# The 20 slabs of w_in multiplied in fp32 instead of as pairs of fp32r halves

## The chip, the cores and the metric

One Trainium2 chip, one core. The metric is the device time of one execution in microseconds. TensorE (PE) multiplies, VectorE (DVE), ScalarE (ACT) and GpSimd (POOL) work element-wise, SyncE (SP) issues most of the loads.

## The reference

One step of a hybrid backbone (one layer, two groups of 128 tokens, width 1024). Both groups share all weights, so the kernel treats them as 256 columns of tokens.

```python
h = _rmsnorm(x, p["norm1_g"]) * (1.0 + sc1) + sh1
z = h @ p["w_in"] + p["b_in"]                  # 1024 x 5120
z_f, z_a, z_b, z_s, z_g = jnp.split(z, cuts, axis=-1)
br_f = _fourier_mix(z_f) @ p["w_four"]
br_c = _conformer_conv(z_a, z_b, ...) @ p["w_conv_out"]
y_s, finals = _s5_bidirectional(z_s, ...)      # two scans
gs = jax.nn.gelu(y_s)
y_s = gs * jax.nn.sigmoid(gs @ p["w_ssm_glu"] + p["b_ssm_glu"])
br_s = y_s @ p["w_ssm_out"]
mixed = (gate_f * br_f + gate_c * br_c + gate_s * br_s) @ p["w_out"]
x = x + g1 * mixed
x = x + g2 * _moe(h2, ...)                     # top 4 of 32 experts
```

## The kernel before

*Stages.* First come the adaLN modulation of the first norm and the tables of the S5 mixer, then the products with w_in, w_four, w_ssm_out, w_conv_out and w_out, with the three mixers between them, then the router, and then the 32 experts, one after the other, whose weights (12 slabs of 1 MB each) stream from HBM.

*Slabs.* Weights arrive as slabs of 1 MB (128 partitions x 2048 fp32) in slots `SL[i]`. `Ring` hands a free slot to the next load in a fixed order (`ring.add`); SP issues the loads in that order, each when its slot has become free (`ring.done`, `ring.give`; a slot named in `ring.drop` does not come back). The loads of w_in (20 slabs of 256 columns, keys `("in", c0)`) alternate with those of w_mod for the later modulation (`("m", ...)`). After the last slab of w_out come the experts' slabs.

*Order.* The stages before the experts are written as generators (`modulate`, `splitter`, `main_products`, `evacuate`, `fourier`, `conv`, `s5`, ...). A planner (`Sched`) with a cost for every operation advances, one instruction at a time, the generator whose next instruction can start soonest, with a small penalty by priority (`PRIO`). This happens while the program is built: on the chip each engine runs its own list in that order.

*The products with w_in.* The operands are fp32r, and each is written as a pair of tiles: `hi` is its copy in fp32r, and `lo` what is left when `hi` is subtracted from it. `modulate` writes h into xT (slot 20) and as the pair `hhi`, `hlo` (slots 4 and 5). `splitter` takes each slab in four units of 128x512: ACT copies a unit to `hi` (fp32r), and DVE or POOL, whichever the planner holds to be free sooner, subtracts for `lo`; `NW = 4` units may be ahead of the products. `main_products` then makes three products (`prod3`) for each block of 128 rows and 128 columns, in PSUM banks 0 and 1 in turn. `evacuate` reads a finished bank: ACT adds the bias, or makes the gates' sigmoid. The branches' weights (w_four, w_conv_out, w_ssm_out, six keys `("pr", i, h)`) and w_out (four slabs) go through the same splitter. All instructions made by `mm` have line 273, all of `tt` line 291, all of `act` line 304, those of `ts` lines 279 and 282.

*Order of the slabs.* Eight slabs of z come first (S5's two, Fourier's two, the convolution's four), then six times two gate slabs and half of one branch's output weights, in the order Fourier, S5, convolution; then w_out. S5 needs, besides its two slabs, tables of which DVE and POOL make parts (`tables_in`, `tables_out`), a scan of 16 steps on DVE whose states ACT copies, and a convolution kernel that goes out to HBM (`Kd`) and comes back in another layout. `fourier` keeps an intermediate in slot 20, after xT is no longer read there; `evacuate` accumulates the gated sum in it.

## Time and profile before

| | us |
|---|---|
| median of 3 runs (lowest, highest) | 1414.85 (1414.38, 1416.57) |
| profiled execution | 1418.22 |
| its span, first to last instruction | 1416.4 |
| busy in it: PE / PE's weight loads | 1243.9 / 655.7 |
| busy in it: DVE / ACT / POOL | 492.4 / 301.5 / 216.0 |
| HBM read | 472.61 MB |
| mean granted TensorE clock | 0.961 of full |

Full clock of TensorE is 2.4 GHz and the other level is 1.2 GHz, so a granted clock of 0.79 over a stretch is a mixture of the two. Busy shares hold for the whole span, in which stages with different limits follow each other. PE's weight loads (PEld) overlap its products. An engine's wait is put down to what ended it.

### The profile page before, as it was taken

Reading aid. Unit: us, or ns where it says so; the run is one execution under the profiler, and the core shown is the slowest. Engines: PE = TensorE matmul, PEld = TensorE weight load, DVE = VectorE, ACT = ScalarE, POOL = GpSimd, SP = SyncE. Lnnn points to the kernel's source line nnn. Section 1 sums busy time; section 2 is a strip of 40 time slices with the busy share of each in tenths; the row PEclk is TensorE's granted clock in tenths of the full one; section 3 lists DMA queues with packets and bytes.
Section 4 is the critical chain, followed back from the end, with each engine's and each line's share of the span. In section 5 each row is a group of like instructions: output and inputs, shape, how many; then the busy total and the mean of one; then the engine's idle time right before and its main releaser. Section 6 shows DMA issues by size and latency. Waiting matters only on the chain. (4 is left out here: it accounts for less than half of the span.)

```text
span 1416.4 us, 19588 instructions
## 1 busy us (share of the span) xinstructions
PE 1243.9 (88%) x7444; PEld 655.7 (46%) x7444; DVE 492.4 (35%) x839; ACT 301.5 (21%) x609; POOL 216.0 (15%) x183
## 2 busy tenths in 40 slices
PE   4596787899999999999989999999999989999994
PEld 3475686789833433334343433333334334343331
DVE  7949898897511111111111111111121111211113
ACT  4454344454311101011100101101011101111011
POOL 4555556565300000000000000000000000000001
PEclk9798899999999999999999999999999999999996
DMA  9563489558799999999998999998999994999990
GB/s 268 193 210 115 144 146 266 188 196 316 290 352 410 416 397 415 416 416 415 417 415 319 407 417 414 415 400 357 416 416 416 416 409 185 413 415 415 414 395 33
DMA packets 124834, 477.08 MB, mean 337 GB/s; under 512 B 11871, under 2 KB 49505, under 8 KB 90864
## 3 DMA queue, kind: packets, MB, share of 16 engines
q1 hardware_dynamic: 121744, 468.25, 85.3%
q0 software_dynamic: 2288, 5.76, 1.2%
q8 instruction: 120, 1.97, 0.6%
q10 hardware_dynamic: 624, 0.63, 0.1%
q14 instruction: 58, 0.48, 0.1%
HBM read 472.61 MB, written 1.61 MB: 335 GB/s over the span
## 5 line engine op out<-in xcount | busy, mean ns | idle before, releaser
L273 PE MATMUL pb<-sl,sl 128*64 128x512 f32 (+4 forms) x5344 | 951.3, 485 | 48.7 <-PEq L1644 13.1
L273 PEld LDWEIGHTS pb<-sl,sl 128*64 128x64 f32 (+2 forms) x5344 | 438.4, 152 | 521.8 <-issue 445.2
L304 ACT ACTIVATE sl<-sl 128x512 fp32r<-128x512 f32 (+4 forms) x211 | 120.8, 588 | 614.2 <-DVE sl L279 496.4
L291 POOL TENSOR_TENSOR sl<-sl,sl 128x512 fp32r<-128x512 f32 (+4 forms) x73 | 121.1, 1667 | 737.5 <-DVE sl L291 607.7
L279 DVE TENSOR_SCALAR sl<-pb 128x512 f32<-128x512 f32 (+1 forms) x35 | 23.7, 676 | 434.7 <-PE pb L273 434.7
L287 DVE SCALAR_TENSOR_TENSOR sl<-pb,wsl,sl 128x512 fp32r<-128x512 f32 x64 | 47.7, 750 | 310.5 <-ACT sl L304 309.3
L291 DVE TENSOR_TENSOR sl<-sl,sl 128x512 fp32r<-128x512 f32 (+3 forms) x107 | 105.6, 1001 | 30.1 <-ACT sl L304 27.7
L304 ACT ACTIVATE sl<-pb 128x512 f32<-128x512 f32 (+6 forms) x125 | 68.5, 585 | 199.2 <-PE pb L273 177.8
L262 PE MATMUL pb<-cst,sl 128*128 128x128 f32 (+2 forms) x354 | 57.4, 296 | 46.0 <-ACT sl L304 15.0
L304 ACT ACTIVATE sl<-pb,wsl 128x512 fp32r<-128x512 f32 x64 | 43.6, 687 | 199.6 <-PE pb L273 196.6
L273 PE MATMUL pb<-sl,PT 128*128 128x512 f32 x256 | 78.0, 428 | 0.5 <-PEq L1644 0.5
L273 PE MATMUL pb<-hb,sl 128*128 128x128 f32 x512 | 68.4, 289 | 7.9 <-DVE hb L291 7.5
L273 PEld LDWEIGHTS pb<-hb,sl 128*128 128x128 f32 x512 | 65.1, 200 | 18.3 <-ACT wsl L304 11.8
L262 PEld LDWEIGHTS pb<-cst,sl 128*128 128x128 f32 (+2 forms) x354 | 43.7, 158 | 63.0 <-issue 26.1
L318 POOL MEMSET sl<- 128x30 f32 (+6 forms) x15 | 2.8, 228 | 374.1 <-PEq L1644 373.8
L287 DVE SCALAR_TENSOR_TENSOR hb<-sl,taps,hb 128x256 f32<-128x256 f32 x90 | 55.5, 664 | 0.6
L273 PEld LDWEIGHTS pb<-sl,PT 128*128 128x128 f32 x256 | 46.2, 201 | 8.0 <-ACT sl L304 1.3
L291 POOL TENSOR_TENSOR sl<-PWT,sl 128x1024 f32<-128x1024 f32 x20 | 43.5, 2190 | 11.1 <-PE pb L273 6.2
L273 PEld LDWEIGHTS pb<-comb,hb 128*128 128x128 f32 x128 | 19.6, 207 | 44.6 <-DVE sl L279 41.9
L291 DVE TENSOR_TENSOR sl<-sl 128x512 f32<-128x512 f32 (+4 forms) x77 | 37.1, 500 | 4.1 <-ACT sl L304 0.5
L273 PE MATMUL pb<-comb,hb 128*128 128x1 f32 x128 | 22.0, 241 | 18.2 <-PEq L1644 16.4
L273 PE MATMUL pb<-ha,selb 128*64 128x512 bf16 (+1 forms) x140 | 21.3, 390 | 16.8 <-PEq L1644 14.4
(176 smaller groups left out, 547.0 us busy)
## 6 DMA issues: line engine op xcount, KB each, us to landing
sl<-w_gate_up SPq DMA_DIRECT2D x256, 1024.0 KB, 14.9
sl<-w_down SPq DMA_DIRECT2D x128, 1024.0 KB, 17.5
sl<-w_mod SPq DMA_DIRECT2D x24, 1024.0 KB, 7.2
sl<-w_in SPq DMA_DIRECT2D x20, 1024.0 KB, 11.1
sl<-w_out SPq DMA_DIRECT2D x4, 1024.0 KB, 6.9
sl<-md POOLq DMA_DIRECT2D x6, 512.0 KB, 6.9
sl<-w_four SPq DMA_DIRECT2D x2, 1024.0 KB
sl<-Kd SPq DMA_DIRECT2D x16, 128.0 KB, 9.2
```

The costliest lines, as they stand in the source:

```text
L262: return sch.op("P", 0.107 * in_.shape[0] / 128, [out], [in_], lambda: te.transpose(out, in_, ident[:in_.shape[0], :in_.shape[0]]))
L273: lambda: te.matmul(out, lhsT, rhs, start=start, stop=stop, skip_group_check=True))
L279: return sch.op(e, c, [o], ap, lambda: ENG[e].tensor_scalar(o, a, s1, None, op0=op0))
L287: lambda: ENG[e].scalar_tensor_tensor(o, a, sc, b, op0=op0, op1=op1))
L291: return sch.op(e, c, [o], [a, b], lambda: ENG[e].tensor_tensor(o, a, b, op=op))
L304: [a] + [x for x in (bias, scale) if hasattr(x, "tensor")], lambda: s.activation(o, a, func, **kw))
L318: return sch.op(e, size(o) * 0.9e-3 + 0.1, [o], [], lambda: ENG[e].memset(o, val))
```

## The change

h is written once, in fp32, into xT: ACT modulates one group of tokens and DVE the other. The pair `hhi`, `hlo` goes, and the splitter passes over the w_in slabs. `main_products` multiplies each w_in slab as it came, in fp32, one product for each block (16 for a slab), and gives the slot back after the last of them. Slot 4 belongs to the ring from the start. Slot 5 takes what the Fourier branch and the gated sum kept in slot 20, and slot 20 goes to the ring after the last product with w_in. `m1_transposes` no longer waits for the first split slab, and the planner's cost of an fp32r product is raised.

```diff
--- before.py
+++ after.py
@@ -264,7 +264,7 @@
         def mm(out, lhsT, rhs, start, stop=False):
             n, m = size(rhs), lhsT.shape[1]
             if lhsT.dtype != F32:
-                c = max(n, m) * 4.17e-4
+                c = max(n, m) * 4.6e-4
             elif m > 64:
                 c = max(n, m) * 1.667e-3
             else:
@@ -433,7 +433,7 @@
             dma("Y", BR[i].rearrange("g d p h -> g d (p h)"), A[n][0].rearrange("d g p h -> g d (p h)"))
         start(0, 1)
         start(2, 3)
-        start(6, 7, 8, 9)
+        start(6, 7, 4, 8, 9)
         dma("G", vrow[0:40], A["b_in"][0].rearrange("(k p) -> k p", p=128))
         for i, n in enumerate(("conv_dw_b", "conv_ln_g", "conv_ln_b", "ssm_d", "b_ssm_glu")):
             dma("G", vrow[40 + 4 * i:44 + 4 * i], A[n][0].rearrange("(k p) -> k p", p=128))
@@ -461,8 +461,6 @@
         R0 = [SL[15][:, 1024:1536], SL[15][:, 1536:2048]]
         modA = sm.tile([128, 2, 8, 2], F32, name="modA")
         pm = sm.tile([128, 4, 2], F32, name="pm")
-        hhi = new(4, F32R)[:, :].rearrange("p (k t) -> p k t", k=8)
-        hlo = new(5, F32R)[:, :].rearrange("p (k t) -> p k t", k=8)
 
         def adaln(key, bk):
             w = ring.get(key)
@@ -533,10 +531,10 @@
                 yield f"xT{b}"
                 for k in (2 * b, 2 * b + 1):
                     for g in range(2):
-                        yield act(hhi[:, k, 128 * g:128 * g + 128], xT[:, k, g], AF.Identity, bias=modA[:, 0, k, g:g + 1],
-                                  scale=modA[:, 1, k, g:g + 1])
-                        yield ts(xT[:, k, g], xT[:, k, g], modA[:, 1, k, g:g + 1], modA[:, 0, k, g:g + 1])
-                    yield tt(hlo[:, k], flat(xT[:, k]), fv(hhi[:, k]), OP.subtract)
+                        if g:
+                            yield ts(xT[:, k, g], xT[:, k, g], modA[:, 1, k, g:g + 1], modA[:, 0, k, g:g + 1])
+                        else:
+                            yield act(xT[:, k, g], xT[:, k, g], AF.Identity, bias=modA[:, 0, k, g:g + 1], scale=modA[:, 1, k, g:g + 1])
                     flags.add(f"hmod{k}")
                 if b == 3:
                     yield tr(PB[2][:, 0:64], vrow)
@@ -810,8 +808,6 @@
         def m1_transposes(js, banks):
             yield from need("xT", "R2", *(("m0",) if js[0] else ()))
             for j in js:
-                if j == 2:
-                    yield "in0"
                 yield f"T{j}"
                 for h in range(2):
                     for i in range(2):
@@ -1036,7 +1032,7 @@
 
         def fourier():
             yield from need("zf", "columns", "M10", "M11", "M12", "M13")
-            UV = SL[20][:, :].rearrange("p (j b c) -> p j b c", j=4, b=2)
+            UV = SL[5][:, :].rearrange("p (j b c) -> p j b c", j=4, b=2)
             for i in range(4):
                 for b in range(2):
                     yield mm(PB[6 + i % 2][:, b * 256:(b + 1) * 256], zf[:, i, b * 128:(b + 1) * 128], cst[:, C_DFT:C_DFT + 256],
@@ -1066,17 +1062,14 @@
             new(21, F32R)
             new(22, F32R)
             n = 0
-            for key in seq + [("out", q) for q in range(4)]:
-                for u in UNITS if key == seq[0] else range(4):
+            for key in [x for x in seq if x[0] == "pr"] + [("out", q) for q in range(4)]:
+                for u in range(4):
                     yield lambda: key in ring.ready and cnt["used"] >= n - NW + 1
                     sl = ring.get(key)
                     if key[0] == "out":
                         src = sl[:, u * 512:(u + 1) * 512].rearrange("p (k c) -> p k c", k=2)
-                    elif key[0] == "pr":
+                    else:
                         src = sl[:, :].rearrange("p (k c) -> p k c", k=4)[:, :, u * 128:(u + 1) * 128]
-                    else:
-                        src = sl[:, :].rearrange("p (k c) -> p k c", k=8)[:, 4 * (u % 2):4 * (u % 2) + 4,
-                                                                          u // 2 * 128:(u // 2 + 1) * 128]
                     b = slice(512 * (n % NW), 512 * (n % NW) + 512)
                     hi, lo = [SL[x][:, b].rearrange("p (k c) -> p k c", k=src.shape[1]) for x in (21, 22)]
                     yield from split(src, hi, lo)
@@ -1084,7 +1077,6 @@
                     n += 1
                     if u == 3:
                         ring.done(key)
-                        flags.add("in0")
 
         def prod3(out, whi, wlo, xhi, xlo, first, last):
             yield mm(out, whi, xhi, first)
@@ -1108,32 +1100,33 @@
                 if key[0] == "pr":
                     _, i, h = key
                     yield f"mix{i}"
-                for u in UNITS if key == seq[0] else range(4):
-                    if key[0] == "in":
-                        c, first, last = u // 2, u == 0, u % 2 == 1
-                        K, xh, xl = range(4 * (u % 2), 4 * (u % 2) + 4), hhi, hlo
-                    else:
-                        c, first, last = u % 2, u % 2 == 0, True
-                        K, xh, xl = range(4), mixhi[i], mixlo[i]
-                    if first:
+                if key[0] == "in":
+                    bk = PB[cnt["bank"] % 2]
+                    yield from bank()
+                    yield lambda: key in ring.ready
+                    w = ring.get(key)[:, :].rearrange("p (k c) -> p k c", k=8)
+                    for n, (k, c) in enumerate((x, c) for x in range(8) for c in range(2)):
+                        if key == seq[0] and c == 0:
+                            yield f"hmod{k}"
+                        yield mm(bk[:, c * 256:(c + 1) * 256], w[:, k, c * 128:(c + 1) * 128], flat(xT[:, k]), n == 0, k == 7)
+                    ring.done(key)
+                    evac.append((key[1], bk))
+                    if key == ("in", seq[-2][1]):
+                        ring.give(20)
+                    continue
+                for u in range(4):
+                    c = u % 2
+                    if c == 0:
                         bk = PB[cnt["bank"] % 2]
                         yield from bank()
                     yield lambda: (key, u) in spl
                     hi, lo = spl.pop((key, u))
-                    for n, k in enumerate(K):
-                        if key == seq[0]:
-                            yield f"hmod{k}"
-                        yield from prod3(bk[:, c * 256:(c + 1) * 256], hi[:, n], lo[:, n], xh[:, k], xl[:, k], first and n == 0,
-                                         last and n == 3)
+                    for k in range(4):
+                        yield from prod3(bk[:, c * 256:(c + 1) * 256], hi[:, k], lo[:, k], mixhi[i][:, k], mixlo[i][:, k],
+                                         c == 0 and k == 0, k == 3)
                     cnt["used"] += 1
-                    if key[0] == "in" and u == 3:
-                        evac.append((key[1], bk))
-                    elif key[0] == "pr" and c == 1:
+                    if c == 1:
                         evac.append((key, u // 2, bk))
-                if key == ("in", seq[-2][1]):
-                    new(4)
-                    new(5)
-                    ring.give(4, 5)
             for q in range(4):
                 bk = PB[cnt["bank"] % 2]
                 yield from bank()
@@ -1164,7 +1157,7 @@
                 if len(job) == 3:
                     (_, i, h), q, _ = job
                     m = slice(1024 * h + 512 * q, 1024 * h + 512 * q + 512)
-                    mac = SL[20][:, m]
+                    mac = SL[5][:, m]
                     if i == 0:
                         yield tt(mac, bk[:, :], gat[q])
                     else:
@@ -1173,7 +1166,7 @@
                         if i == ORDER[2]:
                             yield from split(mac, mh[:, m], ml[:, m])
                             if h and q:
-                                ring.give(20)
+                                ring.give(5)
                 elif isinstance(job[0], tuple):
                     q = job[0][1]
                     c = slice(256 * q, 256 * q + 256)
@@ -1745,7 +1738,6 @@
 NR = 1
 GI = 12
 KS = 4
-UNITS = 0, 2, 1, 3
 MA = 0
 COLS = (1536, 1792, 0, 256, 1024, 1280, 512, 768)
 ORDER = (0, 2, 1)
```

## Rows read from the trace of the kernel before

**Rows 1.** The page's second part, 40 equal slices of the span, busy tenths of DVE

```profile
DVE  7949898897511111111111111111121111211113
```

**Rows 2.** Stages: length, PE, PEld, DVE, ACT, POOL busy (count), granted clock, DMA share, GB/s

```profile
60.00:116.00 56.00, 50.33 (x398) 38.98 (x399) 37.06 (x57) 32.07 (x67) 25.02 (x14) 0.91 0.45 146
116.00:180.00 64.00, 42.37 (x301) 37.12 (x303) 58.88 (x82) 26.86 (x57) 32.40 (x16) 0.79 0.42 147
180.00:259.00 79.00, 63.54 (x811) 57.55 (x802) 72.10 (x122) 37.68 (x82) 47.23 (x44) 0.91 0.89 211
259.00:317.00 58.00, 51.64 (x404) 50.16 (x405) 51.28 (x68) 26.25 (x48) 35.71 (x35) 0.94 0.52 177
317.00:373.00 56.00, 53.57 (x425) 52.01 (x424) 36.02 (x43) 26.82 (x56) 29.34 (x26) 0.97 0.83 308
...
440.00:1390.00 950.00, 877.33 (x4423) 362.73 (x4420) 152.90 (x251) 109.72 (x218) 2.56 (x5) 0.99 0.97 395
```

**Rows 3.** PE before 400 us: a group by shape, then runs (start, length, count)

```profile
L273 PE MATMUL pb<-sl,sl 128*128 128x256 f32 x1472 | 204.0, 299 | 24.1 <-DVE sl L291 10.3 <-POOL sl L291 7.8 <-ACT sl L304 5.0
...
116.68 1.89 PE L273 MATMUL pb<-cst,sl 128*128 128x256 f32 x8
...
239.83 11.04 PE L273 MATMUL pb<-sl,sl 128*128 128x256 f32 x70
...
285.11 11.65 PE L273 MATMUL pb<-sl,sl 128*128 128x256 f32 x95
```

**Rows 4.** Groups by shape before 400 us: count, busy us, mean ns, idle before

```profile
L291 DVE TENSOR_TENSOR sl<-sl,sl 128x512 fp32r<-128x512 f32 x74 | 74.9, 1022 | 26.0 <-ACT sl L304 25.5
...
L282 DVE TENSOR_SCALAR sl<-sl,modA 128x128 f32<-128x128 f32 x16 | 10.1, 666 | 0.0
...
L304 ACT ACTIVATE sl<-sl 128x512 fp32r<-128x512 f32 x124 | 75.9, 627 | 64.5 <-PE pb L273 44.3 <-DVE sl L291 11.6 <-POOL hb L291 7.6
...
L291 POOL TENSOR_TENSOR sl<-sl,sl 128x512 fp32r<-128x512 f32 x50 | 75.8, 1518 | 105.7 <-ACT sl L304 75.1 <-DMA sl<-w_mod 15.1 <-DVE hb L287 7.8
```

**Rows 5.** PE's waits from 60 to 373 us: total us, times, longest

```profile
PE pb L273 <- ACT sl L304: 17.2, 6, 11.9
PE pb L273 <- DVE sl L291: 10.3, 6, 3.8
PE pb L262 <- ACT sl L304: 9.3, 3, 8.1
PE pb L273 <- POOL sl L291: 7.8, 6, 4.4
```

**Rows 6.** PE in order of time: start, length, count, idle before and releaser

```profile
63.10 0.66 PE L262 MATMUL pb<-cst,sl 128*128 128x128 f32 x2 [8.09 <-ACT sl L304]
...
130.51 7.88 PE L273 MATMUL pb<-cst,sl 128*128 128x256 f32 x40 [11.94 <-ACT sl L304]
...
165.51 5.85 PE L273 MATMUL pb<-sl,sl 128*128 128x256 f32 x31 [3.39 <-ACT sl L304]
...
201.86 12.69 PE L273 MATMUL pb<-sl,sl 128*128 128x256 f32 x85 [4.43 <-POOL sl L291]
```

**Rows 7.** POOL and DVE in order of time, 117 to 130 us

```profile
117.23 3.65 POOL L291 TENSOR_TENSOR sl<-sl,sl 128x512 fp32r<-128x512 f32 x2
...
118.61 2.82 DVE L291 TENSOR_TENSOR sl<-sl,sl 128x512 fp32r<-128x512 f32 x1
...
123.29 4.42 DVE L291 TENSOR_TENSOR sl<-sl,w 128x128 f32<-128x128 f32 x2
...
129.77 0.60 DVE L291 TENSOR_TENSOR sl<-sl,w 128x128 f32<-128x128 f32 x2
```

**Rows 8.** DVE in order of time, at 52 us

```profile
51.74 4.72 DVE L282 TENSOR_SCALAR sl<-sl,modA 128x128 f32<-128x128 f32 x2
```

**Rows 9.** PE's weight loads' wait from 385 us on, and a stage as rows 2

```profile
PEld pb L273 <- DMA sl<-w_gate_up: 20.3, 38, 1.5
...
370.00:380.00 10.00, 10.00 (x114) 9.18 (x113) 5.43 (x24) 5.23 (x14) 1.78 (x3) 1.00 0.61 242
```

## The prediction

> **What bounds the kernel now.** The page comes first, for where the time lies. Its slices show two stages. In nine of the first ten, some 350 us, VectorE (DVE) is at 7 to 9 tenths; from the twelfth on it is at 1 or 2 [rows 1]. The table of stages sharpens this: from 440 to 1390 us the experts run with TensorE (PE) busy 877 of 950 us and the DMA engines at 0.97, and the edit touches nothing there. In 116 to 259 us DVE is busy 131 of 143 us and PE only 106, and PE's granted clock is 0.79 and 0.91 of full, a mix of 2.4 and 1.2 GHz. In 317 to 373 us it is the other way round: PE 53.6 of 56, DVE 36 [rows 2]. So the mixers before the experts wait mostly for the element-wise engines, and their last 56 us for PE.
>
> The waits are read next, since a busy share says nothing of who is late. Between 60 and 373 us PE is busy 261 of 313 us, so it stands still for 52 [rows 2]. The four largest rows of its waits make 44.6 (one that began before 60 us counts whole): for ACT 17.2 and 9.3, for DVE's L291 10.3, for POOL's L291 7.8 [rows 5]. L291 is the helper that makes the low halves of the splits. The experts begin when this stage ends, so what it gains or loses should be seen at the end.
>
> **The change, part by part.** *Products.* A slab of w_in now needs 2 x 8 x 3 = 48 fp32r products of 256 columns, 960 in 20 slabs; the count 1472 agrees with 960 + 288 (branches) + 192 (w_out) + 32 (GLU, see below) [rows 3]. An uninterrupted run gives their pace: 95 in 11.65 us, 0.1226 us each, so 960 are 117.7 us. Afterwards there are 320 fp32 products of 256 columns. The records show an fp32 product as two (16 GLU products are 32 of the 1472). Its price has two rows. The Fourier products, 8 records in 1.89 us, are 0.236 us a record with the drain of the last one in it: an upper bound. The run of 70 records in 11.04 us holds the 32 of the GLU; less 38 x 0.1226 = 4.66, that leaves 6.38 us, 0.199 a record: a lower bound [rows 3]. 640 records are 127 to 151 us. I take the middle, 0.2175: 139.2 us, or **+21.5** (bounds +10 to +33). All of it is work on PE.
>
> The Trainium skill (FP8 and Floating Point Precision, TensorE Precision Notes) speaks against the change: it has true fp32 as four passes through the array. At the fp32r pace four passes for each product would be 640 x 0.245 = 157 us, +39 instead of +21.5, and the whole sum would come to +1; the rows lie below it [rows 3]. Rival C holds this price.
>
> *Splits.* 80 of the 120 weight units lose their ACT copy and their DVE or POOL subtraction, which cost 0.63 us on ACT and 1.0 on DVE or 1.5 on POOL; the modulation loses 16 of ACT's fp32r activations, half of DVE's 16 scalings of 0.67 us and the eight subtractions for hlo, while ACT scales the other eight in fp32 [rows 4]. Across the stage that is some 50 us of ACT and 80 to 120 us shared by DVE and POOL. Being beside other work it is worth only what PE waits for it: 10.3 + 7.8 = 18.1 us for L291 [rows 5]. A third of the units stay (branches and w_out), but these lie where PE hardly waits; I take **-15** (bounds -10 to -18).
>
> *The start.* PE stands 8.09 us before 63 us, waiting for ACT's copies, which stand behind modulated activations, which wait for DVE's modA [rows 6]. DVE is then doing scalings that leave: two take 4.72 us at 51.74 [rows 8]. Half of the scalings, the hlo subtractions and the first weight splits all go from there. I take **-7** (bounds 0 to -8: the tables fill a DVE that comes free).
>
> *The scan.* PE's longest wait is 11.94 us at 118 to 130, for an ACT copy of the Fourier branch [rows 6]. ACT is in order, and a copy of the S5 scan stands ahead, which waits for DVE. There DVE's two 128x128 additions take 4.42 us at 123 and 0.60 at 129: the first while POOL works too. One split on DVE (2.82 us) and two on POOL (3.65) fall into this gap [rows 7]; they go, 6.5 us, but POOL's tables stay. With DVE freer for the tables too I take **-8** (bounds 0 to -12).
>
> *Clock and remaining ACT waits.* Behind gaps PE runs at the low clock: 31 records in 5.85 us and 85 in 12.69 are 0.189 and 0.149 us instead of 0.1226, 4.3 us lost in these two alone [rows 6]. With half of the waits gone I take **-5** (bounds 0 to -8). The 3.39 us before the first of these runs are again ACT behind DVE: **-3** (bounds 0 to -3.4).
>
> *Slots.* Slot 4 joins the ring from the start; xT's slot 20 goes to it after the last slab and slot 5 after the last accumulation, so by the end it has as many as before. A slab is held until it is multiplied, not until it is split; splits run at most four units (one slab, about 6 us) ahead, so one more slot covers that: 0. If it doesn't, a product waits for its load, up to 5 us. SP's own order of loads stays, with slab loads still behind the S5 kernel's transfers. The transposes of tables 2 and 3 lose a wait for the first split ("in0"), and the planner's fp32r cost rises from 0.107 to 0.118 us per 256 columns: both move the order only, 0 taken, 3 us either way.
>
> The sum: 21.5 - 15 - 7 - 8 - 5 - 3 = **-16.5 us**. The profiled execution is 1418.2 us (1416.4 of span, 1.8 around it), so it would become 1401.7; the median of the three runs is 3.4 lower, 1414.85, which makes **1398**. The bounds taken all one way give -39 or +23; those ends become rivals.
>
> **What passes through.** In the experts PE waits for the landing of w_gate_up only 20.3 us in 38 waits, and at 370 to 380 us the DMA engines stand at 0.61: the free slots had been filled before the experts start [rows 9]. The first expert's loads follow the w_out loads in SP's queue, and these follow PE. So a shorter front stage moves the loads and the experts together.
>
> **The rivals.** *A. As summed, from 3 to 28 us gained:* 1387 to 1412. For it: the waits named are for things that are removed.
>
> *B. PE packs nearly solid, 1370 to 1387, say 1382.* If DVE's freed time also brings the S5 and convolution chains forward, PE is the only limit from 60 to 373 us. Its busy time there is 261 of 313 us; with +21.5 and without some 8 us of low clock it is 275, which is 38 less than 313 [rows 2]. Against it: PE's order is fixed in advance, and the S5 kernel's way through HBM stays.
>
> *C. No change, 1412 to 1418.* Either the fp32 records cost their upper bound (+33, which leaves -5) and a wait for slots takes the rest, or the experts take the gain back because their loads don't start earlier. Against the latter stand the filled slots. Or an fp32 product costs four fp32r ones, 0.490 us, 157 us in all: +39 - 38 = +1, 1416. That is the Trainium skill's rule cited above. The run of 70 records has no room for such a price, so this way has 3 of C's 11 in 100.
>
> *D. Slower, 1418 to 1436, say 1426: PE becomes the bound where it was not.* The 21.5 us are certain and the gaps are not. The mechanism is POOL's tables: DVE's two-input operations stand still while POOL works [rows 7], and POOL's 2 us table operations remain, so the scan, the copies behind it on ACT and PE's 11.9 and 3.4 us persist, and so do the low clock and the start, because tables fill DVE's free time. Then only the split waits go: 21.5 - 15 = +6.5; with the upper price of fp32 +18. It decides as soon as less than 21.5 us of PE's 52 us of waiting and of its low clock disappears. The Trainium skill, SBUF — State Buffer, Who interferes with whom, says that such operations of DVE and POOL exclude each other for a whole instruction; the rows agree, with 4.42 against 0.60 us.
>
> **How the numbers follow.** A 0.56, B 0.14, C 0.11, D 0.19. A change within 0.2% (2.8 us) is about what a measurement of this kernel cannot tell from none: 1412 to 1417.7. So faster is 0.56 + 0.14 = 0.70, same 0.11, slower 0.19. The predicted time is A's, 1398 us. Leaving out the lowest part of B and the upper half of D, the range is 1378 to 1422; A's own range is 1387 to 1412.
>
> **What would show it.** Right: no fp32r record of weights before the branches; some 640 more fp32 records of 0.2 to 0.236 us pace in place of 960 of 0.1226; the first w_in product near 60 us rather than 66.8; DVE's busy time in 116 to 259 us down by 25 us or more; PE's waits in the front below 30 us and its clock there near 1; the first load of w_gate_up about 16 us earlier, and the experts' stretch as long as before. Wrong: a record pace of 0.24 or more, or waits of PE for a w_in load, for the S5 kernel's transfers or for ACT that add up to 35 us again, or an end that doesn't follow the start of the experts.

## The result, and the profile after

The changed kernel takes 1425.2 us (median of four, 1423.8 to 1425.5) against 1414.6 (1413.9 to 1416.6) of the kernel before on the same chip: ratio 1.0071, 95% interval 1.0053 to 1.0088. It is slower, by 10.6 us or 0.7%, where 1398 was forecast, and it lies above the range. The profiled execution has a span of 1423.1 us. The lines that answer to [rows 1] and [rows 2]: the page's slices for DVE, and the stages (length, PE, PEld, DVE, ACT, POOL busy, granted clock, DMA share, GB/s).

```profile
DVE  7929329982531112111211121111112102121114
```

```profile
60.00:116.00 56.00, 51.45 (x325) 35.01 (x325) 26.05 (x23) 19.31 (x40) 24.49 (x12) 0.97 0.55 180
116.00:180.00 64.00, 49.28 (x574) 39.65 (x574) 38.18 (x79) 20.11 (x47) 13.67 (x10) 0.84 0.34 89
180.00:259.00 79.00, 57.07 (x344) 47.42 (x343) 55.52 (x92) 27.57 (x59) 34.97 (x40) 0.85 0.93 246
259.00:317.00 58.00, 54.26 (x321) 48.47 (x320) 50.37 (x87) 16.26 (x29) 21.46 (x26) 0.97 0.62 207
317.00:373.00 56.00, 54.70 (x355) 50.94 (x354) 23.85 (x27) 16.90 (x32) 16.55 (x12) 1.00 0.65 224
```

DVE is busy 93.7 us instead of 131 in 116 to 259. The work did leave. PE, however, is still idle 36.7 of those 143 us, as against 37.1 before, with a clock of 0.84 and 0.85 (0.79 and 0.91 before).

PE's records of this shape before 400 us and the evacuations of two gate slabs by ACT (for [rows 3]), and the groups by shape that are left (for [rows 4]):

```profile
L273 PE MATMUL pb<-sl,sl 128*128 128x256 f32 x1152 | 217.4, 349 | 13.1 <-DVE sl L291 6.7 <-ACT hc L304 6.1 <-POOL sl L291 0.3
```

```profile
342.74 0.84 ACT L304 ACTIVATE hc<-pb,vec 128x256 f32<-128x256 f32 x2 [3.62 <-PE pb L273]
349.64 0.84 ACT L304 ACTIVATE hc<-pb,vec 128x256 f32<-128x256 f32 x2 [6.07 <-PE pb L273]
```

```profile
L291 DVE TENSOR_TENSOR sl<-sl,sl 128x512 fp32r<-128x512 f32 x21 | 20.7, 988 | 33.5 <-ACT sl L304 21.8 <-DMA sl<-w_gate_up 11.7
...
L282 DVE TENSOR_SCALAR sl<-sl,modA 128x128 f32<-128x128 f32 x8 | 8.3, 1072 | 0.1
...
L304 ACT ACTIVATE sl<-sl 128x512 fp32r<-128x512 f32 x44 | 26.8, 627 | 27.6 <-PE pb L273 18.2 <-DVE sl L291 7.5 <-issue 1.0
...
L291 POOL TENSOR_TENSOR sl<-sl,sl 128x512 fp32r<-128x512 f32 x23 | 31.9, 1394 | 56.1 <-ACT sl L304 56.0
```

Of the 1152 records 640 are the fp32 products with w_in, two records each; the other 512 are 480 of fp32r and the 32 of the GLU, which were fp32 before. Two slabs that follow on each other are evacuated 349.64 - 342.74 = 6.90 us apart, and ACT waits for PE before the second: 0.216 a record, 0.431 us a product, 138.0 us for 320 products, 20.3 more than the 117.7 before. The eighty units' splits are gone.

PE's waits (for [rows 5]), PE in order of time (for [rows 6]), and DVE at 43 and 50 us (for [rows 8]):

```profile
PE pb L273 <- ACT sl L304: 14.9, 3, 10.8
PE pb L273 <- DMA sl<-Kd: 12.5, 2, 12.2
PE pb L273 <- DVE sl L291: 6.7, 2, 3.3
PE pb L273 <- ACT hc L304: 6.1, 1, 6.1
PE pb L273 <- ACT vec L304: 2.7, 1, 2.7
```

```profile
61.14 0.60 PE L273 MATMUL pb<-sl,sl 128*128 128x256 f32 x2
...
121.95 3.78 PE L273 MATMUL pb<-cst,sl 128*128 128x256 f32 x8 [3.82 <-ACT sl L304]
...
136.55 8.08 PE L273 MATMUL pb<-cst,sl 128*128 128x256 f32 x40 [10.81 <-ACT sl L304]
...
198.06 0.64 PE L273 MATMUL pb<-sl,sl 128*32 128x128 f32 x4 [12.18 <-DMA sl<-Kd]
...
204.25 2.32 PE L273 MATMUL pb<-sl,sl 128*128 128x256 f32 x10
```

```profile
42.69 4.33 DVE L282 TENSOR_SCALAR sl<-sl,modA 128x128 f32<-128x128 f32 x2
...
50.43 0.60 DVE L282 TENSOR_SCALAR sl<-sl,modA 128x128 f32<-128x128 f32 x2
```

The first product with w_in starts at 61.14 (66.79 before), and of PE's 7.8 us of waiting for POOL's splits 0.3 are left. The gap of the scan is still there, 3.82 and 10.81 us, and the wait for the S5 kernel's way back from HBM (`Kd`) has grown from 5.3 to 12.2. In the kernel before PE had other products to make while the S5 kernel was on its way (85 records from 201.86 us on [rows 6]), and ACT had evacuated two gate slabs by 211 us. Here PE's list has no gate slab in that place: one whose load had been issued at 152.92 us is multiplied only from 204.25 on. ACT's evacuations, the second gate slab before and the first one after:

```profile
209.91 0.84 ACT L304 ACTIVATE hc<-pb,vec 128x256 f32<-128x256 f32 x2
```

```profile
215.28 0.81 ACT L304 ACTIVATE hc<-pb,vec 128x256 f32<-128x256 f32 x2
```

DVE and POOL at the scan (for [rows 7]), SP's load of that gate slab, and DVE from 158 us on, where it stands still twice, for 22.00 and 23.24 us:

```profile
109.68 4.44 DVE L291 TENSOR_TENSOR sl<-sl,w 128x128 f32<-128x128 f32 x2
...
120.56 1.90 DVE L291 TENSOR_TENSOR w<-A8i,sl 128x128 f32<-128x128 f32 x1
122.38 2.01 DVE L291 TENSOR_TENSOR w<-A8r,sl 128x128 f32<-128x128 f32 x1
...
127.38 0.61 DVE L291 TENSOR_TENSOR sl<-sl,w 128x128 f32<-128x128 f32 x2
...
148.41 0.61 DVE L291 TENSOR_TENSOR sl<-sl,w 128x128 f32<-128x128 f32 x2
...
179.96 0.88 DVE L287 SCALAR_TENSOR_TENSOR sl<-pb,vec,ha 128x256 f32<-128x256 f32 x2 [22.00 <-PE pb L273]
...
204.07 1.50 DVE L287 SCALAR_TENSOR_TENSOR sl<-sl,vec,pb 128x128 f32<-128x128 f32 x4 [23.24 <-ACT sl L304]
205.49 0.87 DVE L287 SCALAR_TENSOR_TENSOR sl<-pb,vec,ha 128x256 f32<-128x256 f32 x2
```

```profile
99.62 4.76 POOL L291 TENSOR_TENSOR sl<-PWT,sl 128x1024 f32<-128x1024 f32 x2 [31.27 <-ACT sl L304]
...
120.34 3.90 POOL L291 TENSOR_TENSOR sl<-PWT,sl 128x1024 f32<-128x1024 f32 x2
124.32 2.47 POOL L291 TENSOR_TENSOR sl<-sl,sl 128x1024 f32<-128x1024 f32 x1
```

```profile
152.92 0.38 SPq L256 DMA_DIRECT2D sl<-w_in  x1
```

The scan runs from 107 to 149 us. Its single operations take 2 us while POOL makes tables, which it does from 99.6 to 126.8, and 0.3 after. Later, the evacuation of the last z slab (205.49, `sl<-pb,vec,ha`) stands in DVE's list behind that of S5's output y (204.07, `sl<-sl,vec,pb`), which waits for the S5 kernel's round trip. That slab's products had been done by 185.9. In the kernel before the order was the other way round, z first and y 47 us later, and the convolution's taps filled the round trip. The same two evacuations there, DVE in order of time:

```profile
179.01 0.87 DVE L287 SCALAR_TENSOR_TENSOR sl<-pb,vec,ha 128x256 f32<-128x256 f32 x2
...
225.72 1.26 DVE L287 SCALAR_TENSOR_TENSOR sl<-sl,vec,pb 128x128 f32<-128x128 f32 x3 [3.60 <-PE pb L262]
```

PE's weight loads from 385 us on, and the stretch 370 to 380 (for [rows 9]):

```profile
PEld pb L273 <- DMA sl<-w_gate_up: 19.0, 40, 1.5
```

```profile
370.00:380.00 10.00, 9.46 (x80) 9.26 (x79) 4.64 (x7) 4.36 (x11) 6.39 (x5) 1.00 0.34 121
```

The experts' first gather on PE starts at 396.04 instead of 383.41, +12.6, and the rest of the span is 1027.1 instead of 1033.0 us; PE's weight loads wait there 19.0 us for w_gate_up where they waited 20.3.

### The profile page after: what moved, and what is told of

Read it like the earlier page. It is cut to its first block, busy times and chain, and to the rows that moved or that the text cites. A ratio compares the mean times of both kernels' runs of the same rounds, so it can differ in the third digit from the quotient of the medians.

```text
span 1423.1 us, 18680 instructions
## 1 busy us (share of the span) xinstructions
PE 1261.2 (89%) x7142; PEld 651.3 (46%) x7142; DVE 433.3 (30%) x777; ACT 255.4 (18%) x521; POOL 160.8 (11%) x149
## 5 line engine op out<-in xcount | busy, mean ns | idle before, releaser
L273 PE MATMUL pb<-sl,sl 128*64 128x512 f32 (+5 forms) x5024 | 962.5, 508 | 44.2 <-PEq L1637 13.4
L273 PEld LDWEIGHTS pb<-sl,sl 128*64 128x64 f32 (+2 forms) x5024 | 431.9, 148 | 530.6 <-issue 440.8
L304 ACT ACTIVATE sl<-sl 128x512 fp32r<-128x512 f32 (+5 forms) x131 | 72.6, 563 | 570.6 <-DVE sl L279 496.4
L291 POOL TENSOR_TENSOR sl<-sl,sl 128x512 fp32r<-128x512 f32 (+4 forms) x44 | 72.7, 1664 | 685.1 <-DVE sl L291 604.3
L291 DVE TENSOR_TENSOR sl<-sl,sl 128x512 fp32r<-128x512 f32 (+3 forms) x48 | 48.7, 1023 | 36.3 <-ACT sl L304 23.4
L291 POOL TENSOR_TENSOR sl<-PWT,sl 128x1024 f32<-128x1024 f32 x16 | 35.7, 2249 | 36.1 <-ACT sl L304 31.3
L291 DVE TENSOR_TENSOR sl<-sl 128x512 f32<-128x512 f32 (+4 forms) x77 | 36.1, 487 | 4.5 <-DVE sl L287 0.5
## 6 DMA issues: line engine op xcount, KB each, us to landing
sl<-w_gate_up SPq DMA_DIRECT2D x256, 1024.0 KB, 14.6
sl<-Kd SPq DMA_DIRECT2D x16, 128.0 KB, 10.6
```

What stands on the lines that cost most here:

```text
L273: lambda: te.matmul(out, lhsT, rhs, start=start, stop=stop, skip_group_check=True))
L291: return sch.op(e, c, [o], [a, b], lambda: ENG[e].tensor_tensor(o, a, b, op=op))
L304: [a] + [x for x in (bias, scale) if hasattr(x, "tensor")], lambda: s.activation(o, a, func, **kw))
```

## The experiments

Each run was timed beside the kernel before on its chip. A result is given as the median time, its ratio to that kernel with the 95% interval, and "start", the first gather of the experts on PE, which comes from the trace of one execution.

**The order of the loads.** First theory: the last z slab loads too late, behind `Kd`. It fell. In the first run the w_mod slabs come behind the z slabs, in the second the S5 kernel's table waits for the last z slab's load:

```diff
-MA = 0
+MA = 8
```

> The changed kernel, with the w_mod slabs of the later modulation placed in the ring behind the eight z slabs instead of between them. Theory of the order: the time was lost because the last z slab is loaded only after the S5 kernel's transfers (at 189.4 us), so that DVE stands still for 45 us; with the slabs in front the convolution's input is ready near 180 us instead of 205, DVE's two long waits (22.0 and 23.2 us) go, and the time falls from 1425 by 10 to 18 us, to 1407 to 1415. Theory of the price: the 19 to 20 us which the fp32 products add on PE are the loss; PE stays as busy and waits elsewhere, and the time stays within 4 us of 1425.

1434.8 us, ratio 1.0139 [1.0100, 1.0177], start 404.4. That is worse, although z is evacuated at 192.3, before y: PE's longest wait for ACT at the scan is now 26.0 us. Why it grew was not followed.

```diff
+            yield lambda: ("in", COLS[-1]) in ring.ready or "za" in flags
```

> The changed kernel, with the S5 convolution kernel's products (and with them its 32 transfers on SP) held until the load of the last z slab has been issued. Theory of the order: the convolution starts some 15 to 25 us earlier, the S5 branch up to 10 us later, and the time falls by 5 to 15 us, to 1410 to 1420. Theory of the price: within 4 us of 1425.

1424.3 us, 1.0057 [1.0040, 1.0074], start 395.6. Nothing moved: the last z slab's load had been issued at 118 us in the changed kernel already. The load at 189.4, which the theory took for it, is a gate slab's.

**Less work, and part of the change.** One run makes 14 of each slab's 16 products (the last 128 rows of h and w_in are left out, so that the routing differs and only the part before the experts can be compared):

```diff
-... (x, c) for x in range(8) for c in range(2) ...
+... (x, c) for x in range(7) for c in range(2) ...
-... n == 0, k == 7)
+... n == 0, k == 6)
```

> The changed kernel without the last 128 of the 1024 rows of h in the products with w_in: 14 of 16 products a slab, 280 instead of 320, so that PE spends about as long on them as before (280 x 0.427 = 120 us against 118). The output lacks that part. Theory of the price: 17 us less on PE, so the time falls by 13 to 17 us, to 1408 to 1412. Theory of the order: the loads keep their places and the convolution is still late, so no more than 6 us are won, 1419 to 1425.

1421.4 us, 1.0040 [1.0022, 1.0057]; start 370.1, 26 us earlier, for 17 us less of PE. The plan had changed with the cost: z comes at 181.1, ahead of y, and DVE's stand-stills of 22 and 23 us are gone. This says that order counted, not only price; it does not separate the two. The other run is the kernel before with the 8 z slabs alone in fp32. To make room it also starts the splitter only after the first mixing, hands slot 21 to the ring once x has been read from it, and moves the Fourier branch's intermediate to slot 22:

```diff
+                if key in seq[:8]:
+                    ... (as the changed kernel's branch for "in")
-            for key in seq + [("out", q) for q in range(4)]:
+            for key in seq[8:] + [("out", q) for q in range(4)]:
...
```

> The kernel before with the 8 z slabs alone multiplied in fp32; the 12 gate slabs are split into pairs as before, from a slot of their own, with the splitter started after the first mixing. Theory of price: 8 slabs by 0.97 us, +8 us on PE, with the gate slabs' splits kept: experts start at about 383 + 5 to 10, time 1418 to 1425. Theory of order: depends on where the evacuation of the last z slab falls against that of y; if z stays ahead (before 190), time 1405 to 1416.

1438.3 us, 1.0163 [1.0135, 1.0190], start 402.4: worse than the whole change, and neither theory had it. z is at 187.7, ahead of y, but the taps, which share DVE with the gates' splits, last until 305 us (281 in the changed kernel). Why this plan spreads them so far stays open, and with the splitter's late start the run does not tell what fp32 in the z slabs alone would cost. A first form of it (1476.3 us, 1.0426 [1.0378, 1.0473]) loaded a slab over x in slot 21, so it worked on other values; nothing is read from it.

**The order of DVE's list.** z ahead of y, by a line in the S5 stage, or by a truer price for the reads of `Kd` in the plan:

```diff
-            yield "M3"
+            yield from need("M3", "za")
```

> The changed kernel, with one line more: the S5 kernel's second stage is not planned until the conv's input (za) is planned, so that VectorE's list has the evacuation of the last z slab and the first taps ahead of the evacuation of y. Theory of order (VectorE stands still 23.2 us behind an evacuation that waits for the round trip of the S5 kernel through HBM, with the last z slab's products long done): za is evacuated near 186 instead of 205.5, VectorE's wait of 23.2 us is gone, the experts start 5 to 15 us before 396.0, time 1408 to 1420. Theory of price (the fp32 products cost PE some 20 us in any order, and PE is the bound): the experts start within 4 us of 396 and the time stays within 4 us of 1425.

1421.0 us, 1.0044 [1.0022, 1.0067], start 391.5. z is at 181.9, and DVE's wait of 23 us is gone, but two of PE's waits stay:

```profile
PE pb L273 <- DMA sl<-Kd: 11.3, 1, 11.3
PE pb L273 <- ACT hc L304: 5.9, 1, 5.9
```

```diff
+            n *= 4 if src.tensor.name[:2] == "Kd" else 1
```

> The changed kernel with one number of its planner changed: a read of the S5 kernel from HBM counts four times its bytes (about what 1.47 us per read in the trace is against 0.36 in the plan). Theory of order: the plan puts the evacuation of the last z slab ahead of that of y by itself, the 23.2 us wait is gone, the experts start 5 to 15 us earlier than 396.0, time 1408 to 1420. Theory of price: within 4 us of 1425.

1420.3 us, 1.0022 [1.0002, 1.0042], start 389.0. z is at 187.1; here the plan also put a gate slab ahead of the S5 kernel's products, and PE's wait for `Kd` is 2.9 us, but its waits for ACT's copies grow from 15.8 to 27.5. The two runs bring 4.5 and 7.0 us of the 12.6 at the experts' start, and both times lie just above the range of the theory of order: order is a part of the loss, not all of it. The control is the same price in the kernel before:

> The kernel before with the same number of its planner changed, as control. Theory of order: its round trip already lies after the evacuation of the last z slab (176 to 180, against 186.7 to 214), so the new price has little to mend: within 4 us of 1414.6. Theory of price says the same; a gain of more than 5 us here would mean that the planner's price is a separate matter that the change did not bring.

1417.8 us, 1.0009 [0.9992, 1.0026], start 382.5: there is no gain there.

**The scan's gap.** ACT's copies of the scan's states moved behind the scan:

```diff
-                yield copy(SH[0:64, :, :, c], prev[0:64])
-                yield copy(SH[64:128, :, :, 15 - c], prev[64:128])
...
+            for r in range(2):      # after the loop over c
+                yield copy(SH[0:64, r, :, 1:16], E[0:64, 0:15, r].rearrange("p c m -> p m c"))
+                yield copy(SH[64:128, r, :, 0:15], E[64:128, 14::-1, r].rearrange("p c m -> p m c"))
```

> The changed kernel; ScalarE's 32 small copies of the S5 scan's states, which stand in its list between the scan's steps, are made in six copies behind the scan. Same values. Theory of the scan gap (PE's waits of 3.8 and 10.8 us at 118 to 137 us are for a ScalarE copy of the Fourier branch that stands behind those small copies, and these behind VectorE's slow scan steps): the two waits fall to under 4 us in all, and the experts start 6 to 12 us before 396.0, time 1411 to 1419. Rival (PE is held there by something else as well, or what is won before 140 us is lost again in the wait for the S5 kernel's round trip and behind the evacuation of y): the waits go, but those for the S5 kernel and on VectorE's list grow by as much, the experts start within 3 us of 396, time 1422 to 1427.

1426.6 us, 1.0076 [1.0051, 1.0101], start 394.6, as the rival had it. PE in order of time in this run:

```profile
159.65 0.64 PE L273 MATMUL pb<-sl,sl 128*32 128x128 f32 x2 [20.83 <-DVE sl L279]
```

The two waits for ACT are gone, and PE waits 20.8 us for DVE itself, whose work for the S5 kernel's table comes behind the same slow scan. ACT only passed DVE's lateness on. With the price of `Kd` as well:

> The changed kernel with both: the planner's price of the S5 kernel's reads four times higher (in the run of it alone the experts started at 389.0) and the scan's state copies behind the scan. If the two losses are of different places, the gains add: experts start at 376 to 384, time 1402 to 1412, below the kernel before. If PE is the bound and its products the whole price, the experts start within 3 us of 389 and the time stays at 1417 to 1421.

1426.2 us, 1.0080 [1.0055, 1.0106], start 395.2: the gains don't add, and that of the price is gone too, which neither theory had. A run meant to hold POOL's tables back until the scan is done (a flag in the plan) told nothing: POOL's list had nothing else in that stretch, and it ran them at 98.8 us as ever:

> The changed kernel; GpSimd's share of the second set of tables waits until the scan is planned, so that GpSimd stands still while VectorE does the scan's steps. Theory that GpSimd's work slows VectorE's steps: the pairs of additions of 2.6 to 4.4 us fall to 0.6, the scan ends some 10 us earlier than 142, and PE's wait of 10.8 us falls below 5. Rival (the scan's steps are slow of themselves): the 2 us steps stay. The tables come later, so the S5 kernel's transfers start later than 165.7, by 5 to 20 us; the time may go either way, 1410 to 1435.

1425.1 us, 1.0063 [1.0041, 1.0085], start 396.2. (The scan that the theory puts at 142 ends at 149 in the changed kernel.)

**What PE's work costs.** The first product of each w_in slab is made three times, and the plan counts the two more as free:

> The changed kernel; the first fp32 product of every slab of w_in is made three times in place of once (the second and third overwrite the first, the values stay), at a cost of nothing in the plan, so that the order of all else stays. 40 more fp32 products by the 0.43 us of the trace are 17 us more on PE. Theory that PE's work passes one to one to the experts' start where PE is busy, and is swallowed where it waits: of the 17 us, those in 60 to 116 and 140 to 186 us count, some are swallowed by the waits for the S5 kernel and for ScalarE; experts start 8 to 15 us after 396, time 1430 to 1440. Theory that PE's time is of no account, because another chain sets the end: within 3 us of 396, time 1422 to 1428.

1433.6 us, 1.0113 [1.0074, 1.0151], start 400.9. 80 more records, 17 us at their pace, moved the experts by 4.8, between the two theories: PE's idle time before them fell from 47.2 to 39.3 us, and its clock rose from 0.92 to 0.94. The waits swallowed a good part of the added work.

**POOL's tables.** All of the second set of tables on DVE:

```diff
-                         ("out", tables_out("V", Mtmp[0], js[1])), ("out", tables_out("G", Mtmp[1], js[1])),
+                         ("out", tables_out("V", Mtmp[0], js[1])),
```

> The changed kernel; all of the second set of S5 tables is made on VectorE, none on GpSimd. Theory that GpSimd's tables slow the scan: no pair of additions of 2.6 to 4.4 us is left among the scan's steps, the scan ends near 130 where it ended at 149, PE's waits for ScalarE at 118 to 137 us fall from 14.6 to under 7. VectorE then does some 15 us more of tables. In the plan VectorE's list also has the last z slab ahead of y. Experts start 8 to 18 us before 396, time 1408 to 1418. Rival (the second engine was worth its slowing; the tables come later and the S5 kernel with them, transfers start after 170): experts start within 4 us of 396, time 1421 to 1430.

**1392.8 us (1392.0 to 1397.3), ratio 0.9852 [0.9820, 0.9883], start 363.6.** It beats both kernels, and by more than either theory had. Its scan, z and y on DVE, its stage 116 to 180 as above, and PE's longest wait:

```profile
104.33 0.61 DVE L291 TENSOR_TENSOR sl<-sl,w 128x128 f32<-128x128 f32 x2
...
127.46 0.61 DVE L291 TENSOR_TENSOR sl<-sl,w 128x128 f32<-128x128 f32 x2
...
164.25 0.88 DVE L287 SCALAR_TENSOR_TENSOR sl<-pb,vec,ha 128x256 f32<-128x256 f32 x2 [8.12 <-PE pb L273]
...
198.96 3.03 DVE L287 SCALAR_TENSOR_TENSOR sl<-sl,vec,pb 128x128 f32<-128x128 f32 x8 [10.07 <-ACT sl L304]
```

```profile
116.00:180.00 64.00, 63.96 (x685) 52.02 (x684) 51.41 (x87) 20.59 (x45) 11.42 (x10) 1.00 0.62 172
```

```profile
193.29 5.13 PE L273 MATMUL pb<-sl,sl 128*32 128x128 f32 x66 [12.66 <-DMA sl<-Kd]
```

Every step of the scan is short, it ends at 128 instead of 149 us and DVE makes the tables behind it, and PE runs 116 to 180 us without a gap at full clock. The largest wait that is left is that for `Kd`. Its plan is another one too: z stands ahead of y, and a gate slab ahead of the S5 kernel's products. With the price of `Kd` as well:

> The same with the price of the S5 kernel's reads four times higher in the plan as well. If the two losses add, experts start at 376 to 384 and the time is 1402 to 1412, below the kernel before; if one hides the other, as with the copies, 386 to 392 and 1416 to 1421.

1396.7 us, 0.9879 [0.9849, 0.9909], start 369.2: there is no further gain, and both ranges, set before the run above was known, were too high. The controls are the kernel before with the tables on DVE, without and with that price:

> The kernel before with all of the second set of S5 tables on VectorE, as control. There VectorE has the splits of w_in to do as well (busy 131 of 143 us in 116 to 259), so the tables come on top of a full engine: theory says that it wins little or loses, experts start at 380 to 390, time 1412 to 1424. If it wins as much as the changed kernel does (8 to 18 us), GpSimd's tables are a loss that both kernels have, and the change's own price is untouched by it.

1404.9 us, 0.9924 [0.9896, 0.9951], start 373.7. It wins too, 9.7 us at the start, more than the theory had: POOL's tables are a loss in both kernels.

> The kernel before with both: tables on VectorE alone and the price of the S5 kernel's reads four times higher. Control for the run with both: 1412 to 1424 by the same reasoning. The difference of the two runs with both edits is the price of the change in a plan that costs its waits better: if it is negative, the fp32 weights win there what they lost here.

1412.1 us, 0.9971 [0.9949, 0.9993], start 379.2. The price costs 5.5 us at the start and 7.2 in time here, so it is no cure, only another order.

**Order or POOL?** Since the fastest run differs in its plan as well, that plan was kept next, and POOL was given 12 useless multiplications (`idle_pool`, cost 0 in the plan, output read by nobody):

```diff
...
+            for _ in range(12):
+                yield sch.op("G", 0.0, [Mtmp[1]], [a, b], lambda: gp.tensor_tensor(Mtmp[1], a, b, op=OP.mult))
...
```

> The run with all tables on VectorE (experts at 363.6, 1392.8 us), with the same plan, and 12 multiplications of 128x1024 on GpSimd into a buffer that nobody reads, from the time on when GpSimd made its tables in the changed kernel. If GpSimd's work slows VectorE's scan: steps of about 2 us are back while it lasts, the scan ends 10 to 20 us later than 127.5, PE waits 8 us or more again between 100 and 150, experts start at 372 to 390, time 1401 to 1418. If the other order of the plan was all: scan steps of 0.3 us, experts within 2 us of 363.6, time 1390 to 1396.

1404.1 us, 0.9934 [0.9912, 0.9956], start 374.2: 10.6 us at the start, 11.4 in time, for work that nothing waits for. POOL, DVE and PE in this run:

```profile
87.07 26.13 POOL L833 TENSOR_TENSOR sl<-PWT,sl 128x1024 f32<-128x1024 f32 x12 [20.37 <-ACT sl L304]
```

```profile
105.20 4.01 DVE L291 TENSOR_TENSOR sl<-sl,w 128x128 f32<-128x128 f32 x2
109.25 1.97 DVE L291 TENSOR_TENSOR w<-A8i,sl 128x128 f32<-128x128 f32 x1
...
136.52 0.61 DVE L291 TENSOR_TENSOR sl<-sl,w 128x128 f32<-128x128 f32 x2
```

```profile
124.35 8.38 PE L273 MATMUL pb<-cst,sl 128*128 128x256 f32 x40 [5.84 <-ACT sl L304]
```

The slow steps and PE's wait for ACT are back, and the scan ends 9 us later, although only the last 9 us of POOL's work fell into it. DVE works through this stretch in the same order as in the run without this work, so order is not the reason. Last, the thrice-made products in the fastest run:

> The run with all tables on VectorE, with the first fp32 product of every slab of w_in made three times, as in the run with that edit alone: 40 more products, 17 us on PE. If PE is the bound once its waits are gone, nearly all of it reaches the experts: start at 374 to 381, time 1403 to 1410. If the waits for the S5 kernel (12.7 us) and the low clock behind them still swallow most: start at 366 to 370, time 1394 to 1400.

1405.3 us, 0.9930 [0.9900, 0.9960], start 376.5: 12.9 of the 17 us arrive now, where 4.8 did before. With most of the gaps closed, three quarters of PE's added work reach the experts.

## Why the prediction was wrong

The stretch from 60 us to the experts' start divides into PE's busy time, in which a low clock shows as longer products, and its idle time. The table has both for the main runs, with the mean granted clock in that stretch (all us but the clock; the times are medians, each on its own chip):

| kernel | start | busy | idle | clock | time |
|---|---|---|---|---|---|
| before | 383.4 | 271.5 | 52.0 | 0.91 | 1414.6 |
| changed | 396.0 | 288.8 | 47.2 | 0.92 | 1425.2 |
| changed, price of `Kd` | 389.0 | 287.4 | 41.7 | 0.94 | 1420.3 |
| changed, tables on DVE | 363.6 | 278.2 | 25.4 | 0.96 | 1392.8 |
| the same, POOL's useless work | 374.2 | 283.6 | 30.7 | 0.95 | 1404.1 |
| before, tables on DVE | 373.7 | 271.7 | 42.0 | 0.92 | 1404.9 |

*Products (+21.5): right.* They cost +20.3 by the pace of the slabs. The 0.490 us a product that the prediction made of the rule of four passes (the Trainium skill, FP8 and Floating Point Precision, TensorE Precision Notes) is above what this trace has, 0.431. *Clock (-5): some -3.* The two terms together were +16.5, and busy time grew by 288.8 - 271.5 = 17.3.

*Start (-7): nearly right.* The first product came 5.7 us earlier. *Splits (-15): three quarters.* PE's waits for L291 in its products fell from 18.1 to 6.7 + 0.3 = 7.0 us. *The later ACT wait (-3): right.* The 3.39 us ahead of 165 us are gone.

*Scan (-8): the first step that failed.* It said that the splits in the gap go, "but POOL's tables stay. With DVE freer for the tables too I take **-8**". What stayed was the cause. The scan's steps run at 2 us as long as POOL makes tables, and the gap is 14.6 us (3.8 and 10.8) where one of 11.9 stood: +2.7 instead of -8. The run with the tables on DVE and the one with useless work on POOL show it from both sides. The rule that rival D named (the Trainium skill, SBUF — State Buffer, Who interferes with whom) agrees with the latter: single steps of 2.0 us beside POOL's work, of 0.3 without.

*Slots and order (0, 3 us either way): the second step that failed, and by as much.* The plan came out in another order. PE's list has no gate slab in the S5 kernel's round trip, and its longest wait for `Kd` grew by 6.9 us. Its wait for the gates' buffers (`hc`), whose evacuations stand behind late taps in ACT's list, grew from 0.7 to 6.1. In DVE's list y stands ahead of the last z slab, which cost a stand-still of 23.2 us. Turning z and y round brought 4.5 us and left PE's two waits nearly as they were (11.3 and 5.9); the price that also moved a gate slab forward brought 7.0. What sets the rest was not taken apart. The prediction looked for this in SP's queue only ("SP's own order of loads stays"). There the difference was small: 9 slabs of w_in instead of 10 went out ahead of the S5 kernel's transfers, and the ninth then lay unused for some 40 us.

The terms as measured, 20.3 - 3 - 11.1 - 5.7 + 2.7 - 3.4 + 6.9 + 5.4, make some +12, and the start moved by +12.6 (the clock's -3 is what the products leave of the busy time). The prediction's own sign of being wrong was met as well: PE's waits for ACT (14.9, 6.1, 2.7 and others of 0.9) and for `Kd` (12.5) add up to 37 us, above its 35.

*Rival D* had the mechanism of the scan and the sign, and its point of decision: the idle time fell by 4.8 us and the low clock's cost by some 3, not by 21.5 together. That it put the time at 1426, within 1 us, is in part luck. Its own sum was +6.5, or +18 with an fp32 price above the measured one; it held the start for unmoved, which came 5.7 us earlier, and it had nothing of the 12.3 us of order.

*What passes through: right in direction.* In the two profiled executions the start moved by +12.6 and the span by +6.7, but that of the kernel before was 3.6 us above its median; the medians moved by +10.6. What the experts took back, if anything, can't be told from this.

The change is not bad in every plan. With the tables on DVE in both kernels it is worth 1392.8 against 1404.9, 12 us (0.9852 / 0.9924 = 0.993): +6.5 us of busy time, -16.6 of idle time. The sum's sign was right there, where the gaps could close. In the plan that was measured busy time rose by 17.3 us and idle time fell by only 4.8.

Of the 32.4 us between the changed kernel and the fastest run, the run with useless work shows 10.6 to be POOL's, with the scan ending 9 us later. In the changed kernel POOL's tables ran beside the scan for 20 us instead of 9, and the scan ended 21 us later than in the fastest run. At the same price for each us of delay that would be some 25 of the 32.4, an estimate from these two runs that none tests. How the rest divides between z ahead of y, the gate slab and the tables behind the scan was not taken apart.

## What to carry to other kernels

A wait that is put down to one engine is worth removing only when the chain behind it is followed to its first cause: here PE waited for ACT, ACT for DVE, and DVE was slowed by POOL, so that freeing DVE and ACT by 59 and 46 us of work over the whole kernel left the gap no shorter. When a change moves work to the engine that sets the end, count its price as certain and each gap that should close as a claim of its own. And where a planner writes in-order lists, a change of costs is a change of order: look for the instruction that now stands behind a transfer, and for ready work that stands behind it.

## What the runs showed of the hardware

DVE's operations of two 128x128 inputs, 0.28 us each alone, took 1.9 to 2.0 us while POOL worked on 128x1024 tables. So a second engine for a share of some element-wise work can make a kernel slower: moving POOL's tables to DVE won 10 us before the change and 32 after it, with what the new plans did included. An fp32 product of 128x128 by 256 columns took 0.431 us, an fp32r one 0.1226, 3.5 to 1. And the S5 kernel's 16 reads of 128 KB from HBM, issued from 174.0 us on, ended the wait at 198.06: 24 us, about 1.5 us each, where the plan had 0.36.
